# Plain products for the first chunks of an MLP, ahead of a 7-product scheme

## The chip, the cores and the metric
One core of a Trainium2 chip runs the whole program in one launch. The metric is the device time of an execution in microseconds (us). TensorE multiplies, VectorE (DVE) and ScalarE (ACT) do the elementwise work, SyncE (SP) issues most transfers. "Columns" are elements along the free dimension of one instruction over 128 partitions.

## The reference, cut to what matters
```python
def sq_relu_mlp(x, w_up, w_down):
    hdn = jax.nn.relu(x @ w_up)
    return (hdn * hdn) @ w_down
...
for i in range(DEPTH):                      # DEPTH = 2, D_MODEL = 1024, D_FF = 4096
    hn = rms_norm(h, norm_mix[i])
    h = h + (stick_breaking_mixer if i % 2 == 0 else rglru_mixer)(hn, ...)
    hn = rms_norm(h, norm_mlp[i])
    h = h + sq_relu_mlp(hn, mlp_w_up[i], mlp_w_down[i])
```
512 tokens and 16 meta tokens ahead of them pass through attention, an MLP, a recurrent block and a second MLP. All of it is float32.

## The kernel before
Activations lie with features on partitions: h is 8 chunks of 128 features by 528 tokens. Every float32 product is made from three faster ones (`mm`, L103): each factor is split (`split`, L63 on ScalarE and L66 on VectorE) into a rounded high half and the low half that is left, and hi x hi, hi x lo and lo x hi are summed in PSUM.

An MLP (`mlp`, L637) runs in four quarters. In each, four pairs of chunks of the hidden layer are made (`up_pair`), and then the down projection adds that quarter into h (`down_ks`, `down_end`). A pair is a 2 x 2 block product: the weights of two chunks (256 columns) by the 1024 features are blocks A11, A12, A21, A22, and the input is split into B11, B12 (features 0 to 511; first and second half of the tokens) and B21, B22 (features 512 to 1023). Where a plain block product takes 8 products of blocks, `up_pair` takes 7 (a Strassen-Winograd scheme): A11 B11, S1 T1, P2 T2, P3 T3, A12 B21, A22 T4 and P4 N22, each of 4 x 3 matmuls of 264 columns (256 in the second MLP, which leaves the meta tokens out). S1 and P2 to P4 are sums of weight blocks (`up_weights`, L662 to L667), T1 to T4 sums of input blocks, and N22 is minus B22. After the products a few VectorE steps put the four results together (L701 to L716), the norm's factor `rstd` is applied, and the squares are split into `hh` and `hl` (L721 to L723).

The input blocks are made by the class `Blocks`, in the projection that comes before: `upper(k)` scales chunk k of h and makes B11 and T1, `lower(k)` scales chunk 4 + k, makes T2, T3 and T4, and splits all of them and B21 and N22. The projections of the attention (first MLP) and of the recurrent block (second MLP) make the chunks of h in the order 4, 5, 0, 1, 6, 2, 3, 7 and 0, 4, 1, 5, 2, 6, 3, 7. So every scheme product needs four finished k of one kind, and the last k waits for chunks 3 and 7. The norm's sum of squares (`Norm.add`, L167) needs all eight chunks; `Norm.finish` sums it over partitions with two matmuls by `ones`, then a square root on ScalarE and a reciprocal on VectorE (L174). In the first quarter two products of the first pair and one of the second are begun ahead of it.

The order of the work is set by a scheduler: it takes the instructions of the program in order of priority, places each on its engine when its operands are due by its own timetable, and gives out tile buffers as they come free. Weight steps have their priority raised by `HP`. Weights come in units of 512 KB into `raw` (3 buffers) and are split into `whi` and `wlo` (2 each). PSUM for the MLP is the pool `mps` of four tiles.

Of the kernel before, what the change touches and what calls it, by code (L numbers as in the profile page):

```python
# [45 lines left out]
def tile_hybrid_trunk(ctx: ExitStack, tc: tile.TileContext, h0, vec, wqk, wv, wo, wob,  # L46
# [136 lines left out]
    class Blocks:  # L183
# [3 lines left out]
        def __init__(self, g0, cols):  # L187
# [3 lines left out]
            b1 = [pair(k, [P, 4, HT], F32R, "xb") for k in range(4)]  # L191
            b2 = [pair(4 + k, [P, 4, HT], F32R, "xn") for k in range(2)]
            self.t = [[b[:, i, :, 0:w] for i in range(2)] for b in big]
            self.op = {f"T{j + 1}": [[b[:, i, j, 0:w] for i in range(2)] for b in big] for j in range(4)}
            self.op["B11"] = [[b[:, i, 0:w] for i in range(2)] for b in b1]
            self.op["B21"] = [[b[:, 2 + i, 0:w] for i in range(2)] for b in b1]
            self.op["N22"] = [[b2[k // 2][:, 2 * (k % 2) + i, 0:w] for i in range(2)] for k in range(4)]

        def scaled(self, c, h_c, x):
            (a, w), _ = self.cols  # L200
            act.activation(out=x, in_=h_c[:, a:a + 2 * w].rearrange("p (b w) -> p b w", b=2), func=AF.Copy,
                           scale=vecs[:, self.g0 + c:self.g0 + c + 1])

        def upper(self, k, h_c):
            w = self.cols[0][1]
            x2 = pair(6, [P, 4, HT], F32, "x2")
            self.x, self.y = x2[:, 0:2, 0:w], x2[:, 2:4, 0:w]
            self.d = pair(7, [P, 4, HT], F32, "t4")[:, :, 0:w]
# [856 lines left out]
```

## Time and profile before

| | |
|---|---|
| three runs | 1221.57, 1222.51, 1223.07 us |
| median | 1222.51 us |
| the profiled execution | 1221.41 us, its span 1219.7 us |
| mean granted TensorE clock | 0.988 of full speed |
| TensorE busy | 1171.8 us, 96% of the span, 8318 matmuls |
| VectorE busy | 892.1 us, 73% |
| ScalarE busy | 642.7 us, 53% |
| chain that ended last | TensorE 83%, VectorE 9%, ScalarE 5% of the span |
| HBM | 86 GB/s over the span |

Matmuls are pipelined, so that a busy TensorE need not be at its peak; how many matmuls a stretch holds tells more. The profile has two places where TensorE's share drops in the middle of the program, 0.7 and 0.8 of a slice near 305 to 366 us and 0.8 near 854 to 885 us. These are the starts of the two MLPs.

### The profile page before, as it was taken

Reading aid. Unit: us, or ns where it says so; the run is one execution under the profiler, and the core shown is the slowest. Engines: PE = TensorE matmul, PEld = TensorE weight load, DVE = VectorE, ACT = ScalarE, POOL = GpSimd, SP = SyncE. Lnnn points to the kernel's source line nnn. Section 1 sums busy time; section 2 is a strip of 40 time slices with the busy share of each in tenths; the row PEclk is TensorE's granted clock in tenths of the full one; section 3 lists DMA queues with packets and bytes.
Section 4 is the critical chain, followed back from the end, with each engine's and each line's share of the span. In section 5 each row is a group of like instructions: output and inputs, shape, how many; then the busy total and the mean of one; then the engine's idle time right before and its main releaser. Section 6 shows DMA issues by size and latency. Waiting matters only on the chain.

```text
span 1219.7 us, 20415 instructions
## 1 busy us (share of the span) xinstructions
PE 1171.8 (96%) x8318; PEld 1105.6 (91%) x8318; DVE 892.1 (73%) x1564; ACT 642.7 (53%) x1066; POOL 12.5 (1%) x30
## 2 busy tenths in 40 slices
PE   8999999999789999999999999999899999999996
PEld 7999999998779999999999999777797988988986
DVE  7887888796898486486486677688974865956844
ACT  6767787685655244244244448666552442533542
POOL 3000000000000000000000000000000000000000
PEclk9999999999979999999999999999999999999998
DMA  6322213042123232332322422223232323223222
GB/s 224 94 72 69 72 36 93 14 124 70 53 70 105 87 121 70 98 111 70 119 89 74 140 82 68 71 87 103 70 105 87 122 72 133 90 88 130 96 69 70
DMA packets 33341, 110.22 MB, mean 90 GB/s; under 512 B 3936, under 2 KB 5984, under 8 KB 33248
## 3 DMA queue, kind: packets, MB, share of 16 engines
q1 hardware_dynamic: 32816, 108.53, 27.5%
q8 instruction: 65, 1.06, 0.4%
q10 hardware_dynamic: 432, 0.39, 0.1%
q14 instruction: 28, 0.23, 0.1%
HBM read 102.49 MB, written 2.10 MB: 86 GB/s over the span
## 4 chain that ended last, share of the span: by engine, by line
PE 83%; DVE 9%; ACT 5%; issue 2%; DMA 1%; SPq 0%; DVEq 0%; ACTq 0%
PE g L103 73%; PE z L103 8%; PE o L103 2%; ACT whi L63 2%; DVE wlo L66 1%; DMA raw<-in_wqk_dram 1%; DVE rstd L174 1%; DVE th L878 1%; ACT r L84 0%; DVE acc L167 0%; DVE i L877 0%; ACT L84 0%; DVE xl L144 0%; ACT th L84 0%; DVE th L912 0%
## 5 line engine op out<-in xcount | busy, mean ns | idle before, releaser
L63 ACT ACTIVATE whi<-raw 128x1024 fp32r<-128x1024 f32 (+1 forms) x146 | 151.7, 1045 | 249.9 <-PE g L103 230.3
L103 PE MATMUL g<-hh,whi 128*128 128x264 f32 (+2 forms) x784 | 231.6, 319 | 3.2 <-ACT whi L63 3.2
L103 PE MATMUL g<-hl,whi 128*128 128x264 f32 (+2 forms) x784 | 232.0, 318 | 0.0
L66 DVE TENSOR_TENSOR wlo<-raw,whi 128x1024 fp32r<-128x1024 f32 (+1 forms) x146 | 176.1, 1210 | 23.0 <-ACT whi L63 22.9
L103 PE MATMUL g<-xt,o 128*128 128x264 f32 (+1 forms) x1024 | 191.3, 286 | 0.9 <-ACT n L696 0.5
L103 PEld LDWEIGHTS g<-xt,o 128*128 128x128 f32 x1024 | 160.3, 191 | 2.0 <-ACT o L63 0.7
L103 PEld LDWEIGHTS g<-hh,whi 128*128 128x128 f32 x784 | 147.5, 189 | 15.9 <-ACT whi L63 5.9
L103 PEld LDWEIGHTS g<-hl,whi 128*128 128x128 f32 x784 | 147.4, 188 | 9.6
L103 PE MATMUL g<-hh,wlo 128*128 128x264 f32 (+2 forms) x784 | 155.9, 318 | 0.0
L103 PEld LDWEIGHTS g<-hh,wlo 128*128 128x128 f32 x784 | 120.3, 188 | 10.1
L738 DVE TENSOR_TENSOR hs<-g,hs 128x528 f32<-128x528 f32 (+1 forms) x62 | 42.6, 696 | 115.9 <-PE g L103 115.9
L103 PE MATMUL g<-xb,whi 128*128 128x264 f32 (+1 forms) x512 | 98.8, 289 | 8.8 <-ACT xb L63 4.3
L103 PEld LDWEIGHTS g<-xb,whi 128*128 128x128 f32 x512 | 80.6, 191 | 11.8 <-ACT xb L63 4.9
L103 PE MATMUL g<-xt,o1l 128*128 128x264 f32 (+1 forms) x256 | 73.2, 286 | 0.1
L103 PE MATMUL g<-xb,wlo 128*128 128x264 f32 (+1 forms) x256 | 73.2, 286 | 0.0
L103 PE MATMUL g<-xt,o2l 128*128 128x264 f32 (+1 forms) x256 | 71.0, 284 | 2.1 <-DVE o2l L66 2.1
L103 PE MATMUL g<-xh,whi 128*128 128x264 f32 x272 | 72.1, 287 | 0.8 <-DVE v L412 0.4
L103 PE MATMUL g<-xl,whi 128*128 128x264 f32 x272 | 72.0, 286 | 0.0
L103 PE MATMUL g<-xm,whi 128*128 128x264 f32 (+1 forms) x384 | 67.3, 322 | 0.1
L721 ACT ACTIVATE hh<-t 128x528 fp32r<-128x528 f32 (+1 forms) x64 | 39.8, 632 | 46.0 <-DVE t L714 45.8
L84 ACT ACTIVATE sp<-sp 128x512 f32<-128x512 f32 (+3 forms) x128 | 62.0, 509 | 1.5
L103 PEld LDWEIGHTS g<-xm,whi 128*128 128x128 f32 x384 | 56.6, 188 | 5.7 <-ACT r L84 0.3
(221 smaller groups left out, 2598.2 us busy)
## 6 DMA issues: line engine op xcount, KB each, us to landing
raw<-in_wup_dram SPq DMA_DIRECT2D x64, 512.0 KB, 3.5
raw<-in_wdn_dram SPq DMA_DIRECT2D x64, 512.0 KB, 3.5
raw<-in_win_dram SPq DMA_DIRECT2D x16, 512.0 KB, 3.4
raw<-in_wqk_dram SPq DMA_DIRECT2D x14, 512.0 KB, 3.7
q<-q SPq DMA_DIRECT2D x16, 264.0 KB, 4.5
raw<-in_wv_dram SPq DMA_DIRECT2D x8, 512.0 KB, 3.5
raw<-in_wo_dram SPq DMA_DIRECT2D x8, 512.0 KB, 3.4
raw<-in_wout_dram SPq DMA_DIRECT2D x8, 512.0 KB, 3.4
```

The source lines that it names most:

```text
L63: act.activation(out=hi, in_=src, func=AF.Copy)
L66: (lo_eng or dve).tensor_tensor(out=lo, in0=src, in1=f32(hi), op=ALU.subtract)
L84: ins = act.activation(out=out, in_=in_, func=func, **kw)
L103: return pe.matmul(out=o, lhsT=lhsT, rhs=rhs, start=start, stop=stop, skip_group_check=True)
L174: dve.reciprocal(out=rstd[:, c0:c0 + w], in_=rstd[:, c0:c0 + w])
L721: act.activation(out=h_, in_=x, func=AF.Square)
L738: dve.tensor_tensor(out=h3, in0=g[:, 0:nb, 0:cw], in1=h3, op=ALU.add)
L878: dve.tensor_tensor_scan(out=ths[n], data0=rs[n], data1=is_[n], initial=0.0, op0=ALU.mult, op1=ALU.add)
```

## The change
The first three pairs of the first MLP and the first pair of the second are computed without the scheme, chunk by chunk (`plain_chunk`): 8 chunks of features x 2 halves of the tokens x 3 matmuls, which need only the scaled blocks B11, B12, B21, B22 themselves. The sums T1 to T4 are made meanwhile (`Blocks.sums`), in the second MLP for k = 0, 1, 2 already in the projection. T4 takes the place of B12 in the tile `xt`, so its halves are written last (`last_sums`). N22 is gone: its product takes B22, and the weight sum P4 changes its sign. The tile `xb` now holds B21 and B22, `xa` B11, and `xt` B12 or T4 and T1, T3, T2. The weight steps of the first scheme pair of the first MLP have a priority raised by 150 instead of 400. The norm is finished after the first plain chunk.

```diff
 class Blocks:
+        def add(self, c, h_c):
+            x, g = self.halves(h_c), self.gain(c)
+            parts = [(x, *self.b2[c - 4])] if c > 3 else [(x[:, i, :], *self.op[n][c]) for i, n in enumerate(("B11", "B12"))]
+            for x, hi, lo in parts:
+                act.activation(out=hi, in_=x, func=AF.Copy, scale=g)
+                dve.scalar_tensor_tensor(out=lo, in0=x, scalar=g, in1=f32(hi), op0=ALU.mult, op1=ALU.subtract)
+
+        def sums(self, k):
...
+            x = pair(6, [P, 4, HT], F32, "x4")[:, :, 0:w]
+            up, low = self.halves(h_chunk(k)), self.halves(h_chunk(4 + k))
+            act.activation(out=x[:, 0:2, :], in_=up, func=AF.Copy, scale=self.gain(k))
+            for i, j in ((2, 1), (3, 0)):
+                act.activation(out=x[:, i, :], in_=low[:, j, :], func=AF.Copy, scale=self.gain(4 + k))
...
+            minus(x[:, 0, :], x[:, 1, :], x[:, 0, :])
+            minus(x[:, 1, :], x[:, 1, :], x[:, 2, :])
+            minus(x[:, 2, :], x[:, 2, :], x[:, 0, :])
+            minus(self.d[:, k, :], x[:, 3, :], x[:, 2, :])
+            split(x[:, 0:3, :], *self.t[k])
+
+        def last_sums(self):
+            for k in range(4):
+                split(self.d[:, k, :], *self.op["T4"][k])
...
 attention_layer, for m in (4, 5, 0, 1, 6, 2, 3, 7):
-            if m in (0, 1, 2, 3):
-                blocks.upper(m, h_chunk(m))
-            if m in (0, 1, 2, 7):
-                blocks.lower(m % 4, h_chunk(m % 4 + 4))
+            blocks.add(m, h_chunk(m))
...
 up_weights
-                with tc.high_priority(HP):
+                with tc.high_priority(HP if p > 3 else ahead):
...
-                    dve.tensor_tensor(out=p4, in0=pq[:, 0:H], in1=a1[:, H:], op=ALU.add)
+                    dve.scalar_tensor_tensor(out=p4, in0=pq[:, 0:H], scalar=-1.0, in1=a1[:, H:], op0=ALU.mult,
+                                             op1=ALU.subtract)
...
 up_pair
-                prod(d, "P4", "N22", False)
+                prod(d, "P4", "B22", False)
...
+            def plain_chunk(f):
+                hi, lo = load_unit(wup[l, f])
+                g = gtile()
+                ks = []
+                for k in (4, 5, 0, 1, 6, 2, 3, 7):
+                    ab = [op[n][k % 4] for n in (("B11", "B12") if k < 4 else ("B21", "B22"))]
+                    ks.append((hi[:, k * P:(k + 1) * P], lo[:, k * P:(k + 1) * P], [x[0] for x in ab], [x[1] for x in ab]))
+                gemm([g[:, i, 0:w] for i in range(2)], cols, ks)
+                if f == 0:
+                    gs = gtile()
+                    rstd = nrm.finish([gs[:, i, 0:w] for i in range(2)], cols)
+                    st["r3"] = rstd[:, c0a:T].rearrange("p (b w) -> p b w", b=2)
+                t = slot(7 + 8 * (f % 2), F32, "tp", T)[:, 0:2 * w].rearrange("p (b w) -> p b w", b=2)
+                dve.scalar_tensor_tensor(out=t, in0=g[:, :, 0:w], scalar=0.0, in1=st["r3"], op0=ALU.max, op1=ALU.mult)
+                square(t, *hidden(f))
...
 for q in range(4):
                 if q == 0:
-                    next(gens[0])
-                    next(gens[0])
-                    next(gens[1])
...
+                    for f in range(2 * plain):
+                        plain_chunk(f)
+                        if f == 0:
+                            for k in todo:
+                                blocks.sums(k)
+                    blocks.last_sums()
+                for j in range(plain if q == 0 else 0, 4):
+                    up_pair(4 * q + j, [hidden(2 * j + i) for i in range(2)])
...
 mixer, for m in (0, 4, 1, 5, 2, 6, 3, 7):
-                (blocks.upper if m < 4 else blocks.lower)(m % 4, h_chunk(m))
+                blocks.add(m, h_chunk(m))
                 nrm2.add(m, h_chunk(m))
+                if m in (4, 5, 6):
+                    blocks.sums(m - 4)
...
-    mlp(0, ALL, ALL, nrm, blocks, done0, gtile)
+    mlp(0, ALL, ALL, nrm, blocks, 3, range(4), 150, done0, gtile)
...
-    mlp(1, HALVES, REAL, nrm, blocks, done1, gtile, last)
+    mlp(1, HALVES, REAL, nrm, blocks, 1, (3,), HP, done1, gtile, last)
```

The scheduler makes a new order of it. TensorE, at the end of the attention projection (`z`, with `xh` of chunk 7 of its input) and the start of the first MLP, before:
```order
L103 MATMUL z<-xh_82,wlo 128x264
L103 MATMUL g<-xb,whi 128x264 x2
L103 MATMUL g<-xb,wlo 128x264
L103 MATMUL g<-xb,whi 128x264 x2
L103 MATMUL g<-xb,wlo 128x264
L103 MATMUL g<-xb,whi 128x264 x2
L103 MATMUL g<-xb,wlo 128x264
L103 MATMUL g<-xt,o_4382 128x264 x2
```
and with the change:
```order
L103 MATMUL z<-xh_82,wlo 128x264
L103 MATMUL g<-xb,whi 128x264 x4
L103 MATMUL g<-xa,whi 128x264 x4
L103 MATMUL g<-xb,whi 128x264 x2
L103 MATMUL g<-xa,whi 128x264 x4
L103 MATMUL g<-xb,whi 128x264 x4
L103 MATMUL g<-xt,whi 128x264 x4
L103 MATMUL g<-xb,whi 128x264 x2
L103 MATMUL g<-xt,whi 128x264 x4
L103 MATMUL g<-xb,wlo 128x264 x2
```
Where parts of the first and second pair stood mixed, whole chunks of 48 matmuls stand now, and the first needs chunk 7 for its last six alone.

VectorE, from the last write of h by the projection (`hs`, the last of them) on, before (`pq`, `raw`, `o1l` are steps of the weight sums, `acc` the norm, `t` and `x` the input's sums):
```order
L604 TENSOR_TENSOR hs<-z,xr 128x264
L219 TENSOR_TENSOR t_4127<-x_4126,t_4127 128x264
L167 TENSOR_TENSOR acc<-acc,sq 128x528
L662 TENSOR_TENSOR pq<-raw 128x512
L66 TENSOR_TENSOR wlo<-raw,whi 128x1024
L66 TENSOR_TENSOR xt<-t_4127,xt 128x792
L663 TENSOR_TENSOR raw<-raw 128x512
L167 TENSOR_TENSOR acc<-acc,sq 128x528
L66 TENSOR_TENSOR xb<-x_4226,xb 128x264
```
and with the change:
```order
L619 TENSOR_TENSOR hs<-z,xr 128x264
L230 TENSOR_TENSOR x_4391<-x_4391 128x264 x2
L66 TENSOR_TENSOR wlo<-raw,whi 128x1024
L230 TENSOR_TENSOR x_4391<-x_4391 128x264
L217 SCALAR_TENSOR_TENSOR xa<-hs,vecs,xa 128x264
L170 TENSOR_TENSOR acc<-acc,sq 128x528
L217 SCALAR_TENSOR_TENSOR xt<-hs,vecs,xt 128x264
L230 TENSOR_TENSOR t_4380<-x_4391 128x264
L217 SCALAR_TENSOR_TENSOR xb<-hs,vecs,xb 128x528
L66 TENSOR_TENSOR xt<-x_4391,xt 128x792
L170 TENSOR_TENSOR acc<-acc,sq 128x528
L230 TENSOR_TENSOR x_4401<-x_4401 128x264 x3
```
The steps of the first pair's weight sums are gone from here, and the inputs' own halves `xa`, `xt` and `xb` are written straight from h, with steps of the sums for k = 1 and 2 between them.

VectorE in the second MLP, around the reciprocals of the norm and the first output step, before:
```order
L219 TENSOR_TENSOR t_9682<-x_9681,t_9682 128x256
L174 RECIPROCAL rstd<-rstd 128x256
L667 TENSOR_TENSOR p_9823<-pq,raw 128x512
L174 RECIPROCAL rstd<-rstd 128x256
L66 TENSOR_TENSOR o2l<-pq,o_9828 128x1024
L66 TENSOR_TENSOR xt<-t_9682,xt 128x3x256
L662 TENSOR_TENSOR pq<-raw 128x512
L663 TENSOR_TENSOR raw<-raw 128x512
L665 TENSOR_TENSOR pq<-raw 128x512
L701 TENSOR_TENSOR u_9791<-g,n_9790 128x256
```
and with the change (`tp` is the first output of the plain chunks, L762; `o1l`, `o2l`, `o3l` are the low halves of the first scheme pair's summed weights; the four `xt<-t` are T4):
```order
L66 TENSOR_TENSOR o2l<-pq,o_9864 128x1024
L177 RECIPROCAL rstd<-rstd 128x256
L66 TENSOR_TENSOR xt<-x_9770,xt 128x3x256
L66 TENSOR_TENSOR o3l<-p_9859,o_9866 128x512
L676 TENSOR_TENSOR pq<-raw 128x512
L177 RECIPROCAL rstd<-rstd 128x256
L66 TENSOR_TENSOR xt<-t_9432,xt 128x256 x4
L66 TENSOR_TENSOR wlo<-raw,whi 128x1024
L677 TENSOR_TENSOR raw<-raw 128x512
L762 SCALAR_TENSOR_TENSOR tp<-g,rstd 128x512 x2
L714 TENSOR_TENSOR u_9883<-g,n_9882 128x256
```
The reciprocals stay among the weight sums. What comes between them and the first output step is now the four T4 and two weight steps, and that output step empties the PSUM tiles of whole finished chunks.

## Rows read from the trace of the kernel before

**Rows 1.** Windows: PE, PEld, DVE, ACT, POOL busy us (instructions), clock, DMA share, GB/s.
```profile
330.00:340.00 10.00, 6.13 (x26) 5.46 (x27) 10.00 (x19) 7.13 (x12) 0.00 (x0) 0.68 0.06 14
340.00:350.00 10.00, 3.92 (x13) 2.54 (x12) 9.59 (x15) 6.98 (x13) 0.00 (x0) 0.67 0.27 94
350.00:360.00 10.00, 10.00 (x67) 9.99 (x68) 8.49 (x15) 3.46 (x6) 0.00 (x0) 0.79 0.31 105
...
380.00:390.00 10.00, 10.00 (x84) 10.00 (x84) 7.66 (x14) 3.94 (x6) 0.00 (x0) 1.00 0.26 92
...
860.00:870.00 10.00, 7.72 (x56) 6.69 (x55) 10.00 (x18) 7.10 (x14) 0.00 (x0) 1.00 0.10 31
870.00:880.00 10.00, 7.79 (x64) 7.39 (x63) 9.83 (x15) 2.92 (x4) 0.00 (x0) 1.00 0.28 98
880.00:890.00 10.00, 10.00 (x87) 10.00 (x86) 9.09 (x17) 6.08 (x9) 0.00 (x0) 1.00 0.25 74
```

**Rows 2.** TensorE's timeline, first MLP: start us, us, instruction, [idle before, releaser].
```profile
329.44 0.28 PE L103 MATMUL z<-xh,wlo 128*128 128x264 f32 x1
330.34 0.48 PE L103 MATMUL g<-xb,whi 128*128 128x264 f32 x2 [0.62 <-DVE hs L604]
...
333.60 0.56 PE L103 MATMUL g<-xb,whi 128*128 128x264 f32 x1 [2.29 <-ACT xb L63]
335.40 0.59 PE L103 MATMUL g<-xb,whi 128*128 128x264 f32 x1 [1.25 <-DVE xb L66]
...
342.88 0.71 PE L103 MATMUL g<-acc,ones 128*128 128x264 f32 x2 [1.89 <-ACT rstd L84]
345.56 0.81 PE L103 MATMUL g<-xb,whi 128*128 128x264 f32 x2 [1.97 <-ACT xb L63]
348.15 0.59 PE L103 MATMUL g<-xb,whi 128*128 128x264 f32 x1 [1.78 <-DVE xb L66]
...
349.84 1.25 PE L103 MATMUL g<-xt,o 128*128 128x264 f32 x4 [0.44 <-ACT o L63]
...
359.52 0.48 PE L103 MATMUL g<-xb,whi 128*128 128x264 f32 x2
```

**Rows 3.** TensorE's timeline, second MLP.
```profile
859.19 0.40 PE L103 MATMUL g<-xb,whi 128*128 128x256 f32 x2
...
867.91 0.70 PE L103 MATMUL g<-acc,ones 128*128 128x256 f32 x2 [1.51 <-ACT rstd L84]
...
874.06 0.38 PE L103 MATMUL g<-xt,o2l 128*128 128x256 f32 x1 [2.05 <-DVE o2l L66]
...
877.31 0.51 PE L103 MATMUL g<-xb,whi 128*128 128x256 f32 x2 [0.15 <-DVE u L701]
```

**Rows 4.** VectorE's timeline, first MLP: spacing of starts gives the prices.
```profile
315.57 1.21 DVE L66 TENSOR_TENSOR wlo<-raw,whi 128x1024 fp32r<-128x1024 f32 x1
316.70 0.70 DVE L167 TENSOR_TENSOR acc<-acc,sq 128x528 f32<-128x528 f32 x1
317.32 0.42 DVE L210 TENSOR_TENSOR t<-x 128x264 f32<-128x264 f32 x1
...
324.14 0.97 DVE L66 TENSOR_TENSOR xt<-t,xt 128x792 fp32r<-128x792 f32 x1
325.04 0.77 DVE L66 TENSOR_TENSOR xb<-x,xb 128x264 fp32r<-128x264 f32 x2
325.73 0.42 DVE L225 SCALAR_TENSOR_TENSOR xn<-x,xn 128x264 fp32r<-128x264 f32 x1
...
346.01 1.80 DVE L174 RECIPROCAL rstd<-rstd 128x264 f32<-128x264 f32 x1
```

**Rows 5.** ScalarE's timeline before the first MLP.
```profile
317.50 0.41 ACT L224 ACTIVATE xn<-x 128x264 fp32r<-128x264 f32 x1
...
329.64 1.06 ACT L63 ACTIVATE whi<-raw 128x1024 fp32r<-128x1024 f32 x1 [0.82 <-PE z L103]
```

More of the change, by code (lines that the diff above doesn't have):

```diff
@@ L105, in gemm, with cut @@
     def gemm(outs, cols, ks, first=True, last=True, before=()):
+        def cut(x, i):
+            return x[i] if isinstance(x, list) else x[:, cols[i][0]:cols[i][0] + cols[i][1]]
         n = len(ks)
@@ L112, in gemm @@
             whi, wlo, xhi, xlo = ks[j]
-            c0, w = cols[i]
             if x == "h":
-                ins = mm(outs[i], whi, xhi[:, c0:c0 + w], first and j == 0, False)
+                ins = mm(outs[i], whi, cut(xhi, i), first and j == 0, False)
                 after(ins, before)
                 before = ()
-                mm(outs[i], whi, xlo[:, c0:c0 + w], False, False)
+                mm(outs[i], whi, cut(xlo, i), False, False)
             else:
-                mm(outs[i], wlo, xhi[:, c0:c0 + w], False, last and j == n - 1)
+                mm(outs[i], wlo, cut(xhi, i), False, last and j == n - 1)
     vecs = const.tile([P, NV], F32, name="vecs")
@@ L190, in __init__ @@
             big = quads([P, 2, 4, HT], F32R, "xt")
[L191 to L196, printed above, removed]
@@ L214, in lower @@
-        def lower(self, k, h_c):
-            x, y, d = self.x, self.y, self.d
-            self.scaled(4 + k, h_c, y)
-            dve.tensor_tensor(out=d[:, 1, :], in0=y[:, 1, :], in1=d[:, 0, :], op=ALU.subtract)
-            dve.tensor_tensor(out=d[:, 2, :], in0=x[:, 1, :], in1=y[:, 1, :], op=ALU.subtract)
-            dve.tensor_tensor(out=d[:, 3, :], in0=y[:, 0, :], in1=d[:, 1, :], op=ALU.subtract)
-            hi, lo = self.t[k]
-            split(d[:, 1:4, :], hi[:, 1:4, :], lo[:, 1:4, :])
-            split(y[:, 0, :], *self.op["B21"][k])
-            hi, lo = self.op["N22"][k]
-            act.activation(out=hi, in_=y[:, 1, :], func=AF.Copy, scale=-1.0)
-            dve.scalar_tensor_tensor(out=lo, in0=y[:, 1, :], scalar=-1.0, in1=f32(hi), op0=ALU.mult, op1=ALU.subtract)
+            b2 = [pair(k, [P, 4, HT], F32R, "xb") for k in range(4)]
@@ new lines, in __init__ @@
+            b1 = [pair(4 + k, [P, 4, HT], F32R, "xa") for k in range(2)]
+            self.t = [[b[:, i, 1:4, 0:w] for i in range(2)] for b in big]
+            self.b2 = [[b[:, 2 * i:2 * i + 2, 0:w] for i in range(2)] for b in b2]
+            self.op = {n: [[b[:, i, j, 0:w] for i in range(2)] for b in big]
+                       for n, j in (("B12", 0), ("T4", 0), ("T1", 1), ("T3", 2), ("T2", 3))}
+            self.op["B11"] = [[b1[k // 2][:, 2 * (k % 2) + i, 0:w] for i in range(2)] for k in range(4)]
@@ new lines, in __init__, with halves, gain @@
+            self.op["B21"] = [[x[:, 0, :] for x in b] for b in self.b2]
+            self.op["B22"] = [[x[:, 1, :] for x in b] for b in self.b2]
+            self.d = None
+        def halves(self, h_c):
+            (a, w), _ = self.cols
+            return h_c[:, a:a + 2 * w].rearrange("p (b w) -> p b w", b=2)
+        def gain(self, c):
+            return vecs[:, self.g0 + c:self.g0 + c + 1]
+        def add(self, c, h_c):
[4 more added lines that the diff above has]
+                dve.scalar_tensor_tensor(out=lo, in0=x, scalar=g, in1=f32(hi), op0=ALU.mult, op1=ALU.subtract)
```

47 lines of the change are left out of this document (17 added, 30 removed).

## The prediction, made blind
> **What bounds the kernel now.** I read the windows first. In the middle of an up projection TensorE is full: 84 matmuls of 264 columns in 10 us, 0.119 us each, at clock 1.00, and 87 of 256 columns in the second MLP, 0.115 us each [rows 1]. Where the first MLP begins it is not: the windows at 330, 340 and 350 us hold 26, 13 and 67 matmuls, while VectorE is busy for 10.00 and 9.59 of 10 us and the granted clock stands at 0.67 to 0.79 [rows 1]. Where the second MLP begins the windows at 860 and 870 us hold 56 and 64, VectorE again full, but the clock stays at 1.00. So in these two places VectorE is the bound, and TensorE elsewhere.
>
> Then TensorE's own timeline, for what ended each wait. The last matmul of the attention projection starts at 329.44; then come waits of 0.62, 2.29, 1.25, 1.89, 1.97, 1.78 and 0.44 us, most of them for an `xb` operand that ScalarE or VectorE had yet to write, one for the norm's square root [rows 2]. The first two big waits stand close together, and behind them TensorE runs at the lower of its two levels, 1.2 GHz instead of 2.4: the four matmuls at 349.84 are (1.25 - 0.59) / 3 = 0.22 us apart [rows 2]. In the second MLP the waits are 1.51 (square root) and 2.05 us (`o2l`, a low half of summed weights) [rows 3].
>
> **What the two starts lose.** First MLP: from 329.44 to 359.52 [rows 2] are 30.1 us, in which the order has 97 ordinary matmuls (11.5 us at 0.119) and two of the norm (0.35 us each, from the spacing in [rows 3] and the two-record rows: 0.7). Lost: 30.1 - 11.5 - 0.7 = 17.9 us. The waits listed add up to 10.2 of it; the other 7.7 is the lower clock. Second MLP: from 859.19 to 877.31 [rows 3] are 18.1 us for 96 matmuls (11.0) and the norm (0.7). Lost: 6.4 us. Together 24.3 us can be won, no more: the rest of the up projections runs without holes before and is left as it is.
>
> **What the change adds.** A pair of chunks costs 7 products x 4 x 3 = 84 matmuls in the scheme and 2 x 8 x 2 x 3 = 96 in the plain way. Three pairs of the first MLP: 36 x 0.119 = 4.3 us; one of the second: 12 x 0.115 = 1.4 us. TensorE is the bound there, so both lie on the path: +5.7. The negated p4 is an operation of the same size on the same engine, and I cost it at nothing: a scalar_tensor_tensor and a tensor_tensor of 264 columns both take 0.42 us [rows 4].
>
> **What it moves, first MLP.** A plain chunk needs only the scaled input and its low half, in the order 4, 5, 0, 1, 6, 2, 3, 7 in which the projection makes them. Prices by the spacing of starts [rows 4]: 1024 columns 1.13, 528 columns 0.62, 264 columns 0.35, 792 columns 0.90, a reciprocal 1.8 us. Two short activations now stand ahead of the weights of the last projections, 0.41 each with some overlap [rows 5]: I add 0.4, so the projection ends near 330.0. VectorE writes chunk 7 of h by 330.5. Its next steps (second order excerpt): two differences 0.7; a low half of weights that must wait for ScalarE's high half, which waits for TensorE to leave the buffer, as at 329.64 [rows 5], so 330.0 + 1.06 + 1.13 = 332.2; a difference and `xa` of chunk 3, 332.9; sum of squares, `xt` of chunk 3 and a difference, 334.2; `xb` of chunk 7, 334.9; then 0.9 + 0.62 + 1.05 + 0.62 to the last sum of squares, 338.1.
> TensorE starts the first chunk 0.6 after the projection, as now [rows 2], at 330.6. It needs `xa` of chunk 3 for its 14th matmul, at 332.2: waits 0.7 to 0.9. `xt` of chunk 3 and `xb` of chunk 7 are early: 33 matmuls take 3.9 us. The chunk ends near 337.2 and the norm's matmul waits for 338.1: 0.9. New waits: 0.4 + 0.6 + 0.9 + 0.9 = 2.8 us. From there the six chunks and the first pair are 45 us of TensorE, and VectorE's list for them comes to 41 us by the same prices (7.9 behind chunk 7's sum, seven low halves of weights 7.9, sums and their splits 4.6, reciprocals 3.6, six chunk outputs 7.3, one pair's weights 5.3 and outputs 4.2), so it keeps up, with 4 us to spare. The halves T4 must wait until the last plain chunk has read B12, whose place they take; TensorE has four products (48 matmuls, 5.7 us) and a few of the down projection before it needs T4, and making them takes about 2 us: nothing. The weights' transfers stand in the same number and order on SP, one of 512 KB per 5.7 us chunk: nothing.
> First MLP: -17.9 + 4.3 + 2.8 = **-10.8 us**.
>
> **Second MLP.** The sums of k = 0, 1, 2 are made inside the output projection, as now, so VectorE is not behind at 859.2, and `xb` of chunk 7 (near 863.2) comes before the 43rd matmul (864.1). The two chunks and the norm end at 859.2 + 11.0 + 0.7 = 870.9, four products of the first pair at 876.4. Then the order puts the next pair's first product. The pool `mps` has four PSUM tiles, held by the two chunks and this pair (the norm's went to the pair), so it waits for the first `tp`. VectorE's list from 863.2 up to it (third excerpt, and the split of p4's sums before it): three weight splits and the pair's sums to 869.4, reciprocal 871.2, splits 872.7, next pair's sum 873.4, reciprocal 875.2, four T4 1.4, low half 1.13, sum 0.62, `tp` 0.62: 879.0. Wait 2.6 us. Second MLP: -6.4 + 1.4 + 2.6 = **-2.4 us**.
>
> **Sum.** -13.2 us. The profiled execution took 1221.4 us, 1.1 less than the median of the three runs; against the median 1222.5 - 13.2 = 1209.3.
>
> **Bounds of what no row shows.** The new waits have no row of their own; none of them at all gives -24.3 + 5.7 = -18.6, that is 1203.9, and twice my 5.4 us gives 1214.7. I take the walk, since its prices are rows.
>
> **Rivals.**
> 1. *The clock still falls.* The first chunk's waits (0.6, 0.9, 0.9) bring the clock down as the waits of 2.29 and 1.25 did [rows 2], and the next 20 us run slow again: +7.7, 1217.0. For it: the same place fell. Against: the second MLP had waits of 1.51 and 2.05 [rows 3] at 1.00 [rows 1], longer than any that I expect. 12%. Beside it: the Trainium skill, TensorE: Matmul & The Clock Gate, section Loop structure matters more than you think, has it that a loop which waits between its matmuls lets TensorE go cold. By that rule alone both starts should have fallen before; the trace agrees in the first MLP and not in the second.
> 2. *PSUM tiles run short in the second MLP.* VectorE is late with `tp` and stays late, so each of the three pairs behind waits 2.6 us for a tile: +5.2, 1214.5. For it: VectorE was busy 9 to 10 of 10 us there before [rows 1]. Against: one scheme pair less takes about 6 us off it. 12%. The Trainium skill, Perfetto Trace Analysis, section Optimization Strategy, reads a gap that repeats on the busiest engine as a sign that the next tile finds no room in SBUF or PSUM. Before, no such gap repeats: each wait names another releaser [rows 3].
> 3. *Slower.* Every plain chunk waits for its own weights: two `whi` buffers, so the high half (1.06) can start only when an earlier chunk ends, and the low half (1.13) stands in VectorE's line behind the sums. If it ends 3.3 us (28 matmuls) after its chunk's start, TensorE waits. With the full 2.2 us on all eight chunks +17.6: 1226.9. It decides from about 1.7 us a chunk. Against: the down projections use one such unit per 48 matmuls, and 380 to 390 us is full [rows 1]; VectorE's list has 4 us to spare. 4%.
> 4. *No new wait*: 1203.9. 6%.
>
> **Numbers.** The forecast has 66%. The range 1204.0 to 1216.0 takes it, rivals 2 and 4 and the part of rival 1 that falls short of its full price. A measurement of this kernel tells 0.2% (2.4 us) from no change: faster 0.94 (all but the slower rival and small cases), same 0.02, slower 0.04.
>
> **What would show it.** In the profile after: some 60 to 80 matmuls per 10 us from 330 on and clock 1.00 throughout; TensorE's waits at the first chunk for an `xa` and for `acc`, under 1 us each; no wait between the plain chunks; in the second MLP one wait of 1 to 4 us for `tp` at the second scheme pair. Clock under 0.9 after 330 would prove rival 1; repeated waits for `whi` or `wlo` rival 3; an end of the first up quarter less than 8 us earlier than before would make the forecast wrong.

## The result, and the profile after

The changed kernel takes **1209.95 us** (median; 1208.55 to 1211.55), the kernel before 1222.79 beside it: ratio **0.9894, 95% interval 0.9883 to 0.9906**. The prediction was 1209.3, range 1204.0 to 1216.0. The profiled execution took 1208.55 us, its span is 1206.8.

The windows of the changed kernel that answer to those of before [rows 1]:

```profile
330.00:340.00 10.00, 7.22 (x53) 6.65 (x53) 9.57 (x19) 8.42 (x15) 0.00 (x0) 1.00 0.16 55
340.00:350.00 10.00, 10.00 (x83) 9.94 (x82) 9.48 (x12) 7.68 (x13) 0.00 (x0) 1.00 0.16 54
350.00:360.00 10.00, 10.00 (x85) 10.00 (x83) 6.16 (x10) 4.17 (x7) 0.00 (x0) 1.00 0.31 105
...
860.00:870.00 10.00, 8.81 (x73) 8.59 (x73) 10.00 (x15) 5.35 (x11) 0.00 (x0) 1.00 0.17 53
```

Where 26, 13 and 67 matmuls stood there are now 53, 83 and 85, the granted clock is 1.00, and VectorE is no longer full from 350 us on. TensorE's timeline of the changed kernel, to be read beside [rows 2] and [rows 3]:

```profile
329.82 0.28 PE L103 MATMUL z<-xh,wlo 128*128 128x264 f32 x1
330.77 0.73 PE L103 MATMUL g<-xb,whi 128*128 128x264 f32 x4 [0.66 <-DVE hs L619]
...
333.44 0.39 PE L103 MATMUL g<-xa,whi 128*128 128x264 f32 x1 [0.85 <-DVE xa L217]
...
339.24 0.71 PE L103 MATMUL g<-acc,ones 128*128 128x264 f32 x2 [1.26 <-DVE acc L170]
...
346.07 0.66 PE L103 MATMUL g<-xb,whi 128*128 128x264 f32 x4
...
351.93 0.66 PE L103 MATMUL g<-xb,whi 128*128 128x264 f32 x4
...
392.03 0.39 PE L103 MATMUL g<-hh,whi 128*128 128x264 f32 x1 [0.42 <-ACT whi L63]
...
850.40 0.63 PE L103 MATMUL g<-xb,whi 128*128 128x256 f32 x4
...
869.60 0.47 PE L103 MATMUL g<-xa,whi 128*128 128x256 f32 x2 [1.19 <-DVE tp L762]
```

The first chunk waits for `hs`, `xa` and `acc`; the chunks behind it follow each other without a hole, 5.86 us apart (346.07, 351.93): 48 matmuls at 0.122. In the second MLP one wait for `tp` is left, and a small one for `o1l` (0.24 us at 883.05).

**Three stretches.** Single executions of one kernel differ by some us before the changed place is reached. So every run is cut at four points: the last matmul of the output projection (329.44 before, 329.82 after), the last addition of the first MLP, the first matmul of the second MLP (859.19 before [rows 3], 850.40 after), and the last addition of the second MLP. The two additions on VectorE, first of the kernel before:

```profile
703.10 0.71 DVE L738 TENSOR_TENSOR hs<-g,hs 128x528 f32<-128x528 f32 x1 [2.37 <-PE g L103]
...
1207.72 0.42 DVE L779 TENSOR_TENSOR hs<-g,hs 128x256 f32<-128x256 f32 x1 [2.04 <-PE g L103]
```

and of the changed one:

```profile
694.31 0.71 DVE L774 TENSOR_TENSOR hs<-g,hs 128x528 f32<-128x528 f32 x1 [2.37 <-PE g L103]
...
1194.89 0.42 DVE L813 TENSOR_TENSOR hs<-g,hs 128x256 f32<-128x256 f32 x1 [2.04 <-PE g L103]
```

The same differences for all runs (us of the profiled execution; the median time beside them; e1 to e12 are the experiments below):

```
               to projection  first MLP   mixer   second MLP   median
before             329.44       373.66    156.09    348.53    1222.79
after              329.82       364.49    156.09    344.49    1209.95
e1 first only      331.14       364.45    156.14    348.59    1214.41
e2 second only     331.14       373.96    156.24    344.29    1219.67
e3 clock           333.33       373.46    156.20    348.35    1223.46
e4 sums late       331.04       362.30    157.75    344.34    1209.87
e5 clock, all      332.57       372.22    157.61    347.50    1221.92
e6 T4 late         330.30       364.38    156.05    345.39    1209.86
e7 two pairs       330.75       362.22    157.72    344.64    1209.47
e8 two in second   332.33       364.37    156.03    344.06    1209.20
e9 one pair        332.39       369.71    157.56    344.60    1218.43
e10 late, two      333.09       365.17    157.63    344.58    1214.10
e11 late, two, two 329.97       367.14    156.04    344.00    1212.15
e12 two and two    332.00       362.30    157.66    344.00    1208.70
```

Runs with the same order of work in a stretch agree there within 0.4 us (first MLP of after, e1, e6, e8: 364.37 to 364.49), except in the mixer and in the first MLP of e10 and e11, which have the same order there and differ by 2.0 us; the last section says what sets them apart. The change is worth 9.2 us in the first MLP and 4.0 in the second: 13.2 together. It was forecast as 10.8 and 2.4, the same sum; but the 10.8 counts 0.4 us by which the projection would end later, and that lies ahead of these stretches. On the same footing the forecast is 11.2 and 2.4.

### The profile page after: what moved, and what is told of

Its sections match the earlier page's. It is cut to its first block, busy times and chain, and to the rows that moved or that the text cites. A ratio compares the mean times of both kernels' runs of the same rounds, so it can differ in the third digit from the quotient of the medians.

```text
span 1206.8 us, 20460 instructions
## 1 busy us (share of the span) xinstructions
PE 1169.0 (97%) x8366; PEld 1106.1 (92%) x8366; DVE 873.5 (72%) x1516; ACT 639.4 (53%) x1062; POOL 13.3 (1%) x30
## 4 chain that ended last, share of the span: by engine, by line
PE 83%; DVE 10%; ACT 4%; issue 2%; DMA 1%; SPq 0%; DVEq 0%; ACTq 0%
PE g L103 73%; PE z L103 7%; PE o L103 2%; DVE wlo L66 2%; ACT whi L63 1%; DVE th L912 1%; DVE rstd L177 0%; ACT r L84 0%; DVE hs L619 0%; DVE acc L170 0%; DVE xl L147 0%; DVE i L911 0%; DVE xt L66 0%; DVE x L230 0%; ACT th L84 0%
## 5 line engine op out<-in xcount | busy, mean ns | idle before, releaser
L63 ACT ACTIVATE whi<-raw 128x1024 fp32r<-128x1024 f32 (+1 forms) x150 | 155.7, 1045 | 263.1 <-PE g L103 245.5
L66 DVE TENSOR_TENSOR wlo<-raw,whi 128x1024 fp32r<-128x1024 f32 (+1 forms) x150 | 180.3, 1207 | 24.5 <-ACT whi L63 24.5
L103 PE MATMUL g<-xt,o 128*128 128x256 f32 (+1 forms) x896 | 163.6, 282 | 0.0
L103 PEld LDWEIGHTS g<-xt,o 128*128 128x128 f32 x896 | 137.7, 188 | 0.4
L103 PE MATMUL g<-xb,whi 128*128 128x264 f32 (+1 forms) x352 | 65.1, 285 | 1.3 <-DVE hs L619 0.7
L103 PE MATMUL g<-xt,o1l 128*128 128x256 f32 (+1 forms) x224 | 63.3, 282 | 0.2 <-DVE o1l L66 0.2
L103 PE MATMUL g<-xt,o2l 128*128 128x256 f32 (+1 forms) x224 | 62.2, 282 | 0.0
L736 ACT ACTIVATE hh<-t 128x512 fp32r<-128x512 f32 (+1 forms) x56 | 34.9, 633 | 45.8 <-DVE t L727 45.8
L103 PEld LDWEIGHTS g<-xb,whi 128*128 128x128 f32 x352 | 53.4, 188 | 2.4 <-DVE u L714 1.3
L103 PE MATMUL g<-xa,whi 128*128 128x264 f32 (+1 forms) x288 | 52.5, 283 | 2.0 <-DVE tp L762 1.2
```

The costliest lines, as they stand in the source:

```text
L63: act.activation(out=hi, in_=src, func=AF.Copy)
L66: (lo_eng or dve).tensor_tensor(out=lo, in0=src, in1=f32(hi), op=ALU.subtract)
L103: return pe.matmul(out=o, lhsT=lhsT, rhs=rhs, start=start, stop=stop, skip_group_check=True)
L736: act.activation(out=h_, in_=x, func=AF.Square)
```

## The experiments

**e1 and e2: one MLP at a time.** The other MLP takes `Blocks` and `mlp` (here `Blocks0`, `mlp0`) from the kernel before, word for word; e1 is shown, e2 does the same with `V_MLP0` and the first call.

```diff
-            blocks = Blocks(V_MLP1, HALVES)
+            blocks = Blocks0(V_MLP1, HALVES)
-    mlp(1, HALVES, REAL, nrm, blocks, 1, (3,), HP, done1, gtile, last)
+    mlp0(1, HALVES, REAL, nrm, blocks, done1, gtile, last)
```

> The first MLP changed, the second as before. By the prediction's terms the first MLP gives 10.8 us: 1222.8 - 10.8 = 1212.0. By the landmarks of the two traces (the ends of the down projections come 8.8 us earlier from the first MLP on) it gives 8.8: 1214.0, and the second MLP the rest. If the two places share something (a gain that one needs from the other), it is neither. TensorE's waits at the first chunk and granted clock 1.00 from 330 us on as in the changed kernel.

> The second MLP changed, the first as before. By the prediction's terms it gives 2.4 us: 1220.4. By the landmarks of the two traces 4.0: 1218.8. With the run of the first MLP alone the two gains should add up to the whole, 12.8 us. In the trace the first MLP's start shows the old waits (2.29, 1.25, 1.89, 1.97, 1.78 us) and the clock of 0.67 to 0.79.

Measured: 1214.41 us, ratio 0.9928 (0.9913 to 0.9943), and 1219.67, ratio 0.9972 (0.9957 to 0.9988). The landmarks hold: 9.2 us from the first MLP and 4.2 from the second in their stretches, within 0.2 us of the whole change, and the two gains in time (9.0 and 3.8 against the kernel before, measured beside each) add up to the whole. The two places show no sign of sharing anything.

e1 shows one thing more. Its second MLP is that of the kernel before, with VectorE's steps in the same order and the same wait of 1.51 us for the square root, but in its execution the clock fell there:

```profile
860.00:870.00 10.00, 8.88 (x56) 8.43 (x57) 9.83 (x13) 3.01 (x5) 0.00 (x0) 0.83 0.33 105
```

```profile
866.61 0.38 PE L103 MATMUL g<-xt,o2l 128*128 128x256 f32 x1 [0.50 <-DVE o2l L66]
...
869.86 0.50 PE L103 MATMUL g<-xb,whi 128*128 128x256 f32 x2 [0.15 <-DVE u L944]
```

The wait for `o2l` was 2.05 us before [rows 3] and is 0.50 here: what TensorE lost by running slow, it waited less. From the first matmul of the second MLP (851.73) to the row at 869.86 are 18.13 us, against 18.12 before.

**e3 and e5: was the lower clock a loss of its own?** The kernel before, with extra matmuls in TensorE's waits. Those of e3 each begin an accumulation beside the first pair's first sum, and its output comes out changed; those of e5 begin none, and its output does not.

```diff
+                    fill = {2: (16, 8), 3: (0, 10)} if l == 0 and p == 0 and left == "A11" else {}
...
+                        if k == 2 and fill:
+                            before = warm(fill[k][0], (last_,))
...
+                        if k in fill:
+                            before = warm(fill[k][1], (i,))
```

`warm(n, ...)` issues n matmuls of 248 columns with `A11` and `B11` of k = 0 into unused columns; e5 calls it for 20 more behind the norm's second matmul.

> The kernel before, with 34 extra matmuls of 248 columns in TensorE's waits of the first pair (16 in that of 2.29 us, 8 in that of 1.25, 10 behind the first of the fourth block), on operands that are there, into columns that nobody reads. Theory 1, the prediction's: the 7.7 us of lower clock were a loss of their own, so with TensorE kept busy the windows from 330 us on show a granted clock of 0.95 to 1.00 and the kernel takes up to 7.7 us less, near 1215. Theory 2: VectorE's list set the end of that stretch whatever the clock was, so the clock stays up but VectorE's waits grow; only the matmuls behind the last wait win, some 21 of them by 0.10 us: 2 us, near 1220.7. Theory 3: the waits did not bring the clock down; then it stays at 0.67 to 0.79 and the time is within 1 us of before.

> As the first clock run, with 20 more extra matmuls behind the norm's second one, ahead of the wait of 2.89 us in which the clock fell there; none of the extra ones starts an accumulation. Measured from the end of the output projection to the start of the second MLP, before took 529.75 us. Theory 1, the prediction's: the 7.7 us of lower clock are a loss of their own: with a granted clock of 0.95 to 1.00 in all windows from the first block on, that stretch takes some 522 us. Theory 2: VectorE's list sets the end of it; only the matmuls behind the last wait (some 21, 0.10 us each) win: 527.5 us, and the kernel about 2 us less than before, the wait for xb being longer by what TensorE saves.

Measured: e3 1223.46 us, ratio 1.0002 (0.9992 to 1.0011); e5 1221.92, ratio 0.9991 (0.9981 to 1.0000). The windows of e3 (the projection ended 3.9 us later there):

```profile
340.00:350.00 10.00, 5.70 (x30) 4.58 (x30) 10.00 (x14) 7.00 (x12) 0.00 (x0) 0.89 0.34 105
350.00:360.00 10.00, 9.62 (x50) 9.02 (x50) 9.58 (x18) 3.75 (x6) 0.00 (x0) 0.60 0.28 105
```

and of e5:

```profile
330.00:340.00 10.00, 8.46 (x65) 7.77 (x64) 9.43 (x20) 7.52 (x13) 0.00 (x0) 1.00 0.01 2
340.00:350.00 10.00, 7.79 (x52) 6.45 (x50) 10.00 (x14) 7.08 (x13) 0.00 (x0) 1.00 0.34 105
350.00:360.00 10.00, 7.70 (x56) 7.10 (x57) 9.48 (x16) 3.73 (x6) 0.00 (x0) 1.00 0.31 105
```

So the waits did bring the clock down: filled, they leave it at 1.00, and in e3 it falls behind the longest wait left open:

```profile
348.27 2.94 PE L103 MATMUL g<-xb,whi 128*128 128x264 f32 x12 [2.89 <-ACT xb L63]
```

But it was worth little. In TensorE's timeline of e5 other waits stand where the slow matmuls were:

```profile
341.65 0.39 PE L104 MATMUL g<-xt,o1l 128*128 128x264 f32 x1 [1.10 <-DVE o1l L67]
...
352.48 0.78 PE L104 MATMUL g<-xt,o 128*128 128x264 f32 x3 [0.98 <-ACT o L64]
...
354.45 0.52 PE L104 MATMUL g<-xt,o 128*128 128x264 f32 x2 [1.19 <-ACT o L64]
```

Two of them are for ScalarE's `o`, but ScalarE had waited for VectorE's sums itself:

```profile
351.37 1.06 ACT L64 ACTIVATE o<-raw 128x1024 fp32r<-128x1024 f32 x1 [1.01 <-DVE raw L668]
...
353.34 1.06 ACT L64 ACTIVATE o<-pq 128x1024 fp32r<-128x1024 f32 x1 [0.52 <-DVE pq L670]
```

With the clock at 1.00 throughout, the first MLP is 1.4 us shorter (372.22 against 373.66), not 7.7. Theory 2 holds: VectorE, at 9.4 to 10.0 of 10 us in all three windows, set when that stretch ends, and TensorE's slowness lay beside its work. (In e5 VectorE's order in the second MLP came out a little different too, that stretch is 1.0 us shorter, and the mixer 1.5 longer.) The ten executions of e5 say the same: their mean granted clock is 0.990 to 0.994, against 0.986 to 0.988 in the kernel before beside them, and the median time is 1.1 us less.

**e4: the differences behind the sums of squares.** `minus` of k = 1, 2, 3 in the first MLP is ordered behind the norm's last addition on VectorE.

```diff
-                dve.tensor_tensor(out=o, in0=a, in1=b, op=ALU.subtract)
+                after(dve.tensor_tensor(out=o, in0=a, in1=b, op=ALU.subtract), before)
...
-                                blocks.sums(k)
+                                blocks.sums(k, (nrm.end,) if l == 0 and k > 0 else ())
```

> The changed kernel with the differences of k = 1, 2, 3 of the first MLP behind the last sum of squares on VectorE. Theory 1: the waits for xa (0.85 us) and for acc (1.26 us) at the first chunk come from these differences, 3.3 us of VectorE's list that stand ahead of the last sum of squares; both go, and the list of 41 us for 45 us still ends in time: 1210.0 - 2.1 = 1207.9, or 2.4 with the matmul's drain. Rival: the sums are then late for the first pair of the 7-product scheme, which waits for xt by about as much as was won: within 0.5 us of 1210.0.

Measured: 1209.87 us, ratio 0.9891 (0.9875 to 0.9908), no difference by the time. But TensorE's timeline of e4 has no wait for `acc` left, and that for `xa` is a third:

```profile
334.02 0.39 PE L103 MATMUL g<-xa,whi 128*128 128x264 f32 x1 [0.27 <-DVE xa L217]
```

and the first MLP is 2.2 us shorter (362.30 against 364.49), as theory 1 had it; the sums came in time. In the profiled execution two things took that back: a fall of the clock in the mixer (157.75 against 156.09; the last section) and a projection that ended 1.2 us later (331.04 against 329.82). What the executions without a profile did is not known.

**e6: T4 behind `tp` in the second MLP.**

```diff
-                split(self.d[:, k, :], *self.op["T4"][k])
+                hi, lo = self.op["T4"][k]
+                act.activation(out=hi, in_=self.d[:, k, :], func=AF.Copy)
+                after(dve.tensor_tensor(out=lo, in0=self.d[:, k, :], in1=f32(hi), op=ALU.subtract), before)
```

> The changed kernel with VectorE's T4 halves of the second MLP behind the tp of the second plain chunk. Theory: the wait of 1.19 us for tp comes from the 1.36 us of T4 halves (and one low half and a sum) ahead of it on VectorE; it goes, and the four T4 halves still come before the pair's sixth product: 1.2 us less between the start of the second MLP and the end (356.4 us in the changed kernel). Rival: T4 is then the late one, and the wait moves to its product: no difference. In time: 1208.8 or 1210.0.

Measured: 1209.86 us, ratio 0.9894 (0.9879 to 0.9909). The wait for `tp` is gone, and TensorE's timeline has three others:

```profile
870.96 0.50 PE L103 MATMUL g<-xb,whi 128*128 128x256 f32 x2 [0.30 <-DVE u L716]
...
875.26 0.47 PE L103 MATMUL g<-xa,whi 128*128 128x256 f32 x2 [0.69 <-DVE t L723]
876.30 0.38 PE L103 MATMUL g<-xt,o2l 128*128 128x256 f32 x1 [0.57 <-DVE o2l L66]
```

1.56 us in place of 1.19; the second MLP is 0.9 longer (345.39), of which these waits are 0.4 and the rest was not traced. The rival was right that the wait would move, but not where to: no wait names T4, and these three name other steps of VectorE. VectorE is full there, and this order, which pulled one step ahead, only moved the wait.

**e7, e8, e9, e12: how many plain pairs.** One number of each call of `mlp`; three and one in the changed kernel.

```diff
-    mlp(0, ALL, ALL, nrm, blocks, 3, range(4), 150, done0, gtile)
+    mlp(0, ALL, ALL, nrm, blocks, 2, range(4), 150, done0, gtile)
```

> The changed kernel with two plain pairs in the first MLP instead of three. TensorE has 12 matmuls less: 1.46 us at 0.122. VectorE has 4.8 us more by the prediction's prices (a pair's sums, weights and outputs 9.5 against two chunks 4.7) and 11.3 us less time for its list before the first scheme pair. Theory 1: its list, 41 us for 45, has room enough for the earlier pair: 1208.5. Rival: the sums, or the first pair's weights, come late, and waits of 2 to 6 us for xt or o2l take the place of what is saved: 1211 to 1214.

> The changed kernel with two plain pairs in the second MLP instead of one. TensorE has 12 matmuls of 256 columns more: 1.4 us. Theory: VectorE has nothing more to catch up with there but the 1.2 us wait for tp, so at the best 1.4 - 1.2 = 0.2 us slower, at the worst 1.4: 1210.2 to 1211.4. Rival: VectorE's lateness costs more than that one wait (small waits further back), and it gains 1 us or more: under 1209.

> The changed kernel with one plain pair in the first MLP instead of three: 24 matmuls less, 2.9 us at 0.122. With two pairs VectorE was full from 350 to 370 us and TensorE too. Theory: with one, VectorE's list (9.6 us more of it than with three pairs, and 22.7 us less time ahead of the first scheme pair) no longer fits, TensorE waits for xt, o1l or o2l, and the first quarter (97.99 us from the end of the output projection to its last addition in the changed kernel, 95.82 with two plain pairs) is longer than with two by 2 us or more. Rival: VectorE still keeps up, and it is shorter again by 1.46: 94.4.

> Two plain pairs in each MLP, nothing else moved. From the end of the output projection to the end of the first MLP two pairs took 362.22 us against 364.49 with three, and in the second MLP two took 344.06 against 344.49 with one. Theory 1: both stay and the kernel takes 1210.0 - 2.3 - 0.4 = 1207.3. Rival: what is won early is taken back by a short fall of the clock in the mixer (0.90 to 0.93 between 750 and 770 us), which both quicker first MLPs showed (the run with late differences, that with two pairs) and the changed kernel did not; it costs some 1.7 us, and the kernel takes 1209.

Measured: e7 1209.47 us, ratio 0.9891 (0.9876 to 0.9906); e8 1209.20, 0.9886 (0.9870 to 0.9903); e9 1218.43, 0.9952 (0.9937 to 0.9966); e12 1208.70, 0.9879 (0.9860 to 0.9899).

With two pairs the first MLP is 2.3 us shorter (362.22): the 1.46 of twelve matmuls, and the wait of 0.42 for `whi` at 392.03 is gone; the rest was not traced. In e7 VectorE is full from 350 to 370 us, and TensorE too; the first of the two windows:

```profile
350.00:360.00 10.00, 10.00 (x84) 10.00 (x83) 10.00 (x14) 7.35 (x14) 0.00 (x0) 1.00 0.42 120
```

With one it is 5.2 longer than with three. TensorE's timeline of e9:

```profile
336.97 0.39 PE L103 MATMUL g<-xa,whi 128*128 128x264 f32 x1 [1.85 <-DVE xa L217]
...
344.97 1.25 PE L103 MATMUL g<-acc,ones 128*128 128x264 f32 x2 [3.46 <-DVE acc L170]
...
359.83 0.48 PE L103 MATMUL g<-xa,whi 128*128 128x264 f32 x2 [1.76 <-DVE tp L762]
```

The weights of the scheme's first pair now stand ahead of `xa` and `acc` on VectorE (steps of L676 and L677 ahead of `xa`; L679, `o1l`, L681 and `o2l` ahead of the last sum of squares). So VectorE's list fits with two pairs and no longer with one; but the big waits came at the first chunk and for `tp`, not at `xt`, `o1l` or `o2l` as the theory had it. Part of the loss is the clock's, which fell behind the 3.46 us:

```profile
340.00:350.00 10.00, 6.54 (x34) 6.11 (x33) 10.00 (x14) 7.40 (x11) 0.00 (x0) 0.68 0.32 104
```

Some 20 matmuls are 0.22 us apart there, an estimated 2 us at most; how much of that the next wait for VectorE (1.76) would have taken anyway is open.

In the second MLP a second plain pair takes the two waits (1.19 and 0.24) away and adds 1.42 us of matmuls. The three executions with two pairs took 344.00 to 344.06, the six with one (after, e2, e4, e7, e9, e10) 344.29 to 344.64: some 0.4 us less, where the theory had 0.2 to 1.4 more. In the whole time that can't be seen. e12 has both gains in its stretches (362.30 and 344.00, 2.7 us together), and in the profiled execution the mixer took 1.6 of them back, as the rival had it. Its interval and that of the changed kernel overlap, so it isn't shown to be faster.

**e10 and e11: late differences with two pairs.** The edits of e4 and e7 together; e11 with two pairs in the second MLP as well.

> Differences behind the sums of squares, and two plain pairs in the first MLP. Theory 1: the two gains add up: from the end of the output projection the first quarter takes 97.99 - 2.3 - 2.2 = 93.5 us, and the kernel 1209.9 - 4.5 = 1205.4 if no short fall of the clock elsewhere takes it back, 1207 with one. Rival: with two pairs less time is left for the postponed differences, the first scheme pair waits for xt of k = 3, and the quarter takes 95 to 97 us.

> As the one before, and two plain pairs in the second MLP. The second MLP took 344.06 us to its last addition with two plain pairs against 344.49 with one, so by theory 0.4 us less than the run before; rival: the difference is no more than what two executions differ by, and the two kernels take the same time.

Measured: 1214.10 us, ratio 0.9915 (0.9900 to 0.9929), and 1212.15, 0.9906 (0.9890 to 0.9923). The two gains, 2.2 and 2.3 us, don't add up: the first MLP of e10 (365.17) is 0.7 us longer than that of the changed kernel, and its first quarter took 99.43 us, more than the rival's 95 to 97. TensorE's timeline of e10:

```profile
364.65 0.39 PE L103 MATMUL g<-xa,wlo 128*128 128x264 f32 x1 [1.11 <-DVE wlo L66]
...
367.56 0.51 PE L103 MATMUL g<-xt,o 128*128 128x264 f32 x2 [1.43 <-ACT o L63]
```

The rival holds in kind, by other operands than it named: the postponed differences meet the first pair's weights on VectorE, and TensorE waits at the first scheme pair instead of at the first chunk. Both changes had spent the same spare time. e11 went against its theory in one stretch and with it in the other: its second MLP is 0.6 us shorter than that of e10 (344.00), and its first MLP, with the same order of matmuls, 2.0 longer (367.14), by a fall of the clock (last section).

## Why the prediction came out right, step by step

**The bound.** That VectorE bounds the two starts is shown for each: at the first, e5 took the clock's part away and won only 1.4 us of what the plain chunks win; at the second, TensorE ran slow in e1 and the start ended no later. That the two gains don't depend on each other is shown by e1 and e2. What is not taken apart: the change also drops N22, moves the input sums and lowers the priority of the first pair's weights, and no run has these without plain chunks.

**The clock.** The text split the 17.9 us into 10.2 of waits and 7.7 of lower clock. The sum was right to use, since the change removes both. But the 7.7 was a remainder, not a reading. Between 329.44 and 359.52 the trace of before has 35 steps of 0.22 us from one matmul to the next, 0.10 above those at 1.00: 3.4 us. Most of the rest lies around the waits, where a step is longer than the idle time named. And with the clock held up, 1.4 us came back.

Rival 1 didn't come: the clock stayed at 1.00 at this start in all six profiled executions with this first chunk (after, e1, e6, e7, e8, e12), with waits of 0.62 to 0.66, 0.84 or 0.85, and 1.26 or 1.27. So its price in the changed kernel is not shown; elsewhere a fall cost 1.6 us (mixer) and 2.0 (e11). The ground given against it was luck of one execution: with the second MLP as before, the clock stayed up in the kernel before and fell in e1.

For the rule of the Trainium skill cited there (TensorE: Matmul & The Clock Gate, Loop structure matters more than you think), e3 and e5 agree: the clock followed the waits, up where they were filled and down behind the wait of 2.89 us. But that section speaks of a long wait between every matmul, and the waits of both starts stand between groups of matmuls, so the text read more out of it than it says. What a fall costs depends on who is the bound meanwhile.

**The first MLP: -10.8 forecast, -9.2 measured.** Its first quarter ends at these rows on VectorE, before:

```profile
435.90 0.71 DVE L738 TENSOR_TENSOR hs<-g,hs 128x528 f32<-128x528 f32 x1 [0.17 <-PE g L103]
```

and after:

```profile
427.81 0.70 DVE L774 TENSOR_TENSOR hs<-g,hs 128x528 f32<-128x528 f32 x1
```

From the projection's last matmul that is 106.46 us with 720 matmuls (336 up, 384 down), and 97.99 with 756: 8.5 us. Two terms were mis-sized:
- The price of a matmul. 84 in a window of 10 us gives 0.119, but a window counts those at its edges that lie partly outside. The spacing is 5.86 / 48 = 0.122. Take 1.4 us for the norm and for the way from the last matmul to its addition (an estimate: 1.0 as in the second MLP below, and 0.3 before, 0.6 after). Then the quarter lost 17.2 us before (106.46 - 87.8 - 1.4) and not 17.9, and the 36 added matmuls cost 4.4.
- The new waits, 2.8 forecast, 2.4 of them behind the projection's end. TensorE's rows show 0.66, 0.85, 1.26 and 0.42: 3.2 in all, and after the change the quarter loses 4.4 (97.99 - 92.2 - 1.4). Each wait costs more than the idle time named: from 329.82 to 330.77 are 0.95, less 0.122 for the matmul 0.83, with 0.66 of it idle. The sum of squares came 1 us later than the walk had it, near 339.1 and not at 338.1. The 0.42 for `whi` at the first down projection wasn't forecast. The wait for `acc` was to be under 1 us by the signs that the text named; it was 1.26.

Ahead of the last sum of squares VectorE's timeline shows where the 1 us is:

```profile
330.55 0.96 DVE L230 TENSOR_TENSOR x<-x 128x264 f32<-128x264 f32 x2
331.42 1.22 DVE L66 TENSOR_TENSOR wlo<-raw,whi 128x1024 fp32r<-128x1024 f32 x1
...
337.13 1.44 DVE L230 TENSOR_TENSOR x<-x 128x264 f32<-128x264 f32 x3 [0.18 <-ACT x L225]
338.49 0.70 DVE L170 TENSOR_TENSOR acc<-acc,sq 128x528 f32<-128x528 f32 x1
```

The five differences, which read and overwrite the same tile, come at 0.44 to 0.45 (0.87 for two, 1.36 for three), where 0.35 had been taken from other steps [rows 4]: half of the 1 us. That it is the shared tile which makes them dearer is not shown. Another 0.27 is a wait for ScalarE's `x`, and the rest lies in the scaled halves `xa`, `xt` and `xb`.

So -17.2 + 4.4 + 4.4 = -8.4; the estimate of 1.4 drops out of this sum. The quarter came 8.5 us earlier; below 8 the text would have called its own forecast wrong. Another 0.7 came in the three later quarters (373.66 - 106.46 = 267.20 us before, 364.49 - 97.99 = 266.50 after); their cause was not looked for.

**The second MLP: -2.4 forecast, -4.0 measured.** The place and the releaser of the new wait were right, its size not: 1.19 and not 2.6. TensorE came to it 0.8 later than forecast (868.4, the forecast moved to this start is 876.4 - 8.8 = 867.6), because 144 matmuls cost 0.118 each and not 0.115 and the norm more than 0.7. VectorE came 0.8 earlier; its timeline:

```profile
860.42 1.74 DVE L177 RECIPROCAL rstd<-rstd 128x256 f32<-128x256 f32 x1
862.09 0.89 DVE L66 TENSOR_TENSOR xt<-x,xt 128x768 fp32r<-128x768 f32 x1
...
868.77 1.28 DVE L762 SCALAR_TENSOR_TENSOR tp<-g,rstd 128x512 f32<-128x512 f32 x2
```

The first `tp` ends near 869.4, not 870.2; a reciprocal of 256 columns is 1.67 by the spacing, where 1.8 had been taken from 264.

With a matmul at 0.118 and the norm at 1.0 the start lost 5.8 us before (18.1 - 11.3 - 1.0), not 6.4. So -5.8 + 1.4 + 1.2 = -3.2. The trace agrees: with as many matmuls left to do, the changed kernel is 19.2 us from its start (850.40 to 869.60) and the kernel before 22.4 (18.12 and 36 matmuls at 0.118). The other 0.8 us came later, in the rest of that up projection and the first down projection, and was not traced.

**Two errors that cancelled.** In the first MLP the gain was 2.0 us smaller than forecast on the same footing (9.2 against 11.2): 0.7 by the price of a matmul, 2.0 by the new waits, less the 0.7 of the later quarters. In the second it was 1.6 larger: 0.8 at the start, where VectorE came that much earlier, and 0.8 behind it. TensorE priced too low made the loss of both starts look larger, and in the second the wait longer, which evened out there. Nothing ties these errors together; that their sum is near nothing is luck, and the forecast of 1209.3 is better than its terms.

**Costed at nothing, and so in the trace:** the negated `p4` (0.69 a piece on VectorE, 0.68 before), the T4 halves of the first MLP and the weights' transfers. No wait of TensorE there names any of them.

**Rivals 2, 3 and 4** didn't come. `tp` is waited for once, no plain chunk waits for its weights, and the waits are not none. The slower side exists, but elsewhere than rival 3 put it: e9, with too few plain pairs, loses at `xa` and `acc` against the changed kernel, though it is still faster than the kernel before.

## What to carry to other kernels

Where one engine is the bound for a while, find how much dearer work the other must do until the first has caught up: two plain pairs were enough here; one makes the stretch 7.5 us longer than two (up to 2 of it by a fall of the clock), three 2.3. Price an instruction by the spacing of starts in an unbroken run, not by a count in a window. Leave no remainder of a sum named after a cause that wasn't counted in rows. A stretch at a low clock is worth only what the engine's slowness adds to the end of that stretch, and a gain of one or two us should be looked for in the stretch where it arises, since the total moves by as much from run to run.

## What was not expected of the hardware

**The same waits, with and without a fall of the clock.** In the mixer TensorE waits twice for 0.91 us. In the changed kernel the clock doesn't mind:

```profile
757.74 0.39 PE L103 MATMUL g<-uh,igh 128*128 128x264 f32 x1 [0.91 <-DVE rec L869]
759.03 0.39 PE L103 MATMUL g<-ul,rgh 128*128 128x264 f32 x1 [0.91 <-DVE ul L66]
...
760.38 2.00 PE L103 MATMUL g<-xm,whi 128*128 128x512 f32 x8
```

In e12, with the same instructions in the same 0.02 us, it falls:

```profile
757.72 0.39 PE L103 MATMUL g<-uh,igh 128*128 128x264 f32 x1 [0.91 <-DVE rec L869]
759.01 0.39 PE L103 MATMUL g<-ul,rgh 128*128 128x264 f32 x1 [0.91 <-DVE ul L66]
...
760.06 0.42 PE L103 MATMUL g<-ul,igh 128*128 128x264 f32 x1
760.28 0.42 PE L103 MATMUL g<-uh,igl 128*128 128x264 f32 x1
```

Behind the second wait the matmuls are 0.22 us apart, 1.2 GHz. In the table the mixer has two times and nothing between: 156.03 to 156.24 us in eight executions, 157.56 to 157.75 in six. The difference, 1.6 us, is the price of one such fall. It doesn't go with the time at which the mixer begins (e12 begins within 0.02 us of the changed kernel). The same happened in the first MLP of e10 and e11, which have the same order of matmuls there. In e10 the clock is 1.00 behind waits of 1.11 and 1.43 us (rows above), in e11 it falls behind the same two (1.14 and 1.43):

```profile
360.00:370.00 10.00, 7.30 (x35) 6.31 (x34) 8.80 (x14) 3.67 (x6) 0.00 (x0) 0.71 0.30 105
```

```profile
364.46 2.51 PE L103 MATMUL g<-xt,o 128*128 128x264 f32 x6 [1.43 <-ACT o L63]
```

The first quarter, in which this lies, took 2.0 us longer in e11 (101.41 against 99.43). The third case is the second MLP of the kernel before and of e1, where the fall cost nothing, because VectorE was the bound.

The Trainium skill (TensorE: Matmul & The Clock Gate, What's actually happening) says that the gate watches in windows that run freely and don't begin anew with a kernel, and that therefore the same kernel has more or fewer slow matmuls from run to run; it says so of a kernel's first matmuls. The traces fit that in the middle of a kernel too, with six mixers caught and eight spared; where a window stood, no trace here shows.

Similar falls stand ahead of the changed place (windows of 10 us at 0.83 to 0.99 between 30 and 50 us in seven of the executions, and one at 0.83 either from 280 or from 310 us on in all but one), and account for part of the spread of 329.4 to 333.3 us there. So in the profiled executions of e4, e7 and e12, gains of 2 to 3 us in their stretches leave hardly anything in the total: the mixer took 1.6 to 1.7 us, and the projection ended 0.9 to 2.2 us later than in the changed kernel's. Whether being quicker makes the fall likelier, six against eight executions don't settle.
